# Depthwise convolution on TensorE with 64 channels doubled in time: four tiles there, three on VectorE

## The chip, the cores and the metric

The kernel runs on one core of one Trainium2 chip. The metric is device time in microseconds (us) of one launch, the median of several runs. Durations inside the kernel come from one profiled execution, whose own time stands beside the median below.

## The reference

Two layers run over 256 latent tokens of width 1024 (batch 1), with 256 context tokens that share the weights. Each layer is a gated feed-forward block, a mixer, and a second feed-forward block; after each of them comes a residual and a LayerNorm. The mixer of layer 0 is attention with pooling; that of layer 1 is the convolution module, and only there does the change lie:

```python
a, g = jnp.split(h @ w_c1 + b_c1, 2, axis=-1)
z = a * jax.nn.sigmoid(g)
z = lax.conv_general_dilated(z, w_dw[:, None, :], window_strides=(1,), padding=[(15, 15)], ..., feature_group_count=1024) + b_dw
z = jax.nn.silu(layer_norm(z, ln_g, ln_b))
return z @ w_c2 + b_c2
```

The middle step is a depthwise convolution: 31 taps over time, each of the 1024 channels by itself, in float32.

## The kernel before

**Weights.** Every large weight is loaded as float32 in pieces of 1 MB (`raw`, three buffers) by DMAs that SyncE issues, and split into a high part on ScalarE (`wh`, line 133) and a low part on VectorE, or for some pieces on GpSimd (`wl`, line 134). Each product is three matmuls on TensorE (lines 196 to 198). A `raw` buffer is loaded again when both parts of its old content have been made.

**Convolution stage (from line 864).** The 1024 channels are eight tiles `j` of 128 channels; channels lie on partitions, the 256 tokens along a row. The first product and `glu` (line 884) fill `zp[:, j, :]`, which has 15 zeros on both sides. Then the tiles part ways:

- `DVE_CONV`, tiles 0, 2, 3, 4: VectorE adds up 31 scaled, shifted copies in PSUM (`dve_tap`, lines 904 and 907).
- `POOL_CONV`, tile 1: ScalarE makes 31 scaled copies (`product`, lines 917 and 921, in buffers `pd`), GpSimd adds them (`add_up`, line 925).
- `PE_CONV`, tiles 5, 6, 7: for each tap ScalarE makes a diagonal matrix `dg` (line 986), and TensorE multiplies it with the shifted row of 256 tokens and adds up in the PSUM tile `pc` (line 987). ScalarE copies `pc` to `cv` with the bias (line 990).

`back(j)` (line 929) transposes a finished tile so that tokens lie on partitions (`cvt`, one PSUM tile for each 128 tokens and each half of the channels, line 935), and VectorE takes statistics of it (`ln_part`, line 299). `BACK` says behind which tap matmul the transposes of which tiles are queued; `back_after(last, 7)` is the last. Then come the mean and variance (line 1001), the inverse root on GpSimd (line 1003), the scaling to `yn` (line 1011), transposes back (line 1018), SiLU into `cv` (line 1020), the split into `XH`, `XL`, and the second product. Three rows `bcr` (bias b_c2), `lnr[0]`, `lnr[1]` are loaded at the start of the stage; lines 994 to 996 scale `bcr` and add it to `lnr[1]`, and lines 1006 and 1007 apply them to the residual `h`.

**Order of the work.** The framework writes out the order of each engine's instructions, and of SyncE's DMAs, ahead of time: of the instructions whose inputs and buffers are ready in its own model of the time, the one that stands first in the program comes first. So an instruction can overtake one that stands ahead of it in the program. On the chip each queue then goes strictly in that order: a waiting instruction holds all behind it. `tc.issue_after(x)` puts instructions behind `x` on the same engine. PSUM tiles are tracked by bank: a write into one part of a tile waits for reads of another part that stand ahead in the program.

Of the kernel before, what the change touches and what calls it, by code (L numbers as in the profile page):

```python
# [9 lines left out]
F32 = mybir.dt.float32  # L10
F32R = mybir.dt.float32r
AF = mybir.ActivationFunctionType
# [4 lines left out]
P = 128  # L17
D = 1024
KT = D // P
SEQ = 256  # L20
# [6 lines left out]
TAPS = 31  # L27
HALO = TAPS // 2
# [3 lines left out]
NSPARE = 4  # L32
HP = 700

DVE_CONV = (0, 2, 3, 4)
POOL_CONV = 1
PE_CONV = (5, 6, 7)
PLO = range(9, 24)

BACK = {(5, 30): (0,), (6, 30): (1, 2, 5), (7, 20): (3, 6), (7, 30): (4,)}  # L40


CO = {}
_n = 0
for _name, _w in (("c", 8), ("cc", 8), ("lng", 48), ("lnb", 48), ("cvg", 8), ("cvb", 8), ("bc1", 16), ("bdw", 8),
                  ("psc", 4), ("sub", 1), ("bad", 9 * 8 * DEPTH)):
    CO[_name] = _n
    _n += _w
# [4 lines left out]
def body(ctx: ExitStack, tc: tile.TileContext, out, a):  # L53
    nc = tc.nc
    act, dve, pool, pe = nc.scalar, nc.vector, nc.gpsimd, nc.tensor
# [12 lines left out]
    def mmt(name):  # L68
        return mmp.tile([P, 512], F32, tag="mm", name=name)

    def trt(name):
        return trp.tile([P, 512], F32, tag="tr", name=name)
# [4 lines left out]
    ident = const.tile([P, P], F32, name="ident")  # L77
# [5 lines left out]
    def col(name, i=0, n=1):  # L83
        return cols[:, CO[name] + i: CO[name] + i + n]
# [13 lines left out]
    taken = [0]  # L98
# [23 lines left out]
    def spare(pool, q0, n, tag, **kw):  # L122
        for q in range(q0, q0 + n):
            alt[q] = lambda name: pool.tile([P, 1024], F32R, tag=tag or name[:2] + "x", name=name, **kw)
# [12 lines left out]
    def wnext(ahead=AHEAD):  # L137
        q = taken[0]
        taken[0] += 1
        pump_load(qmap[q][0] + 3)  # L140
        with behind_x():
            pump_split(q + ahead)
        return ready[q]
# [152 lines left out]
    def ln_part(key, i, n, src):  # L296
        if key not in bst:
            bst[key] = tp.tile([P, n, 6], F32, tag="bst", name=f"bst{key}")
        dve.bn_stats(bst[key][:, i, :], src)
# [177 lines left out]
    with ExitStack() as st0:  # L477
# [29 lines left out]
        for ch in range(2):  # L507
            cs = slice(ch * 4, ch * 4 + 4)
            for v in range(2):
# [3 lines left out]
                for q in range(4):  # L513
                    aw = sp.tile([P, 1024], F32, tag="aw", name=f"aw{v}{ch}{q}", bufs=8)
                    nc.sync.dma_start(aw, a["wst"][v, ch, q // 2, :, (q % 2) * 1024:(q % 2 + 1) * 1024])
                    for kk in range(2):
                        k = q * 2 + kk
                        src = aw[:, kk * 512:(kk + 1) * 512]
# [17 lines left out]
                tr = trt(f"sttr{v}{ch}")  # L536
# [55 lines left out]
    with ExitStack() as st2:  # L592
# [44 lines left out]
        for g, win in enumerate(WINS):  # L637
            src = (SA, SB)[g % 2]
            o = 8 - win // 2
# [224 lines left out]
    with ExitStack() as st3:  # L864
        cp = st3.enter_context(tc.tile_pool(name="cp", bufs=1))
        c2 = st3.enter_context(tc.tile_pool(name="c2", bufs=2))
        xmp[:] = c2, 2
        bcr = cp.tile([P, D], F32, name="bcr")
        nc.sync.dma_start(bcr, a["b_c2"][0].partition_broadcast(P))
        lnr = [cp.tile([P, D], F32, name=f"clnr{j}") for j in range(2)]  # L870
        for j, key in enumerate(("ln_g", "ln_b")):
            nc.sync.dma_start(lnr[j], a[key][1, 0].partition_broadcast(P))
        G = mrow[1, 5, 0]
        wd = cp.tile([P, 8 * TAPS], F32, name="wd")
        nc.sync.dma_start(wd, a["wdw"])
        warm = cp.tile([P, 1], F32, name="warm")
        zp = cp.tile([P, KT, SEQ + 2 * HALO], F32, name="zp")
        for o in (0, HALO + SEQ):
            pool.memset(zp[:, :, o:o + HALO], 0.0)
        cv = cp.tile([P, KT, SEQ], F32, name="cv")  # L880
        taps = []
# [9 lines left out]
        pds = []  # L891
        last_add = [None]

        def dve_tap(j, tap):
            w = wd[:, j * TAPS + tap:j * TAPS + tap + 1]
            if tap == 0:
                i = DVE_CONV.index(j)
                if i % 2 == 0:
                    accs[j] = adp.tile([P, 512], F32, tag="ad", name="acc01") if i == 0 else mmt(f"acc{j}")
                else:  # L900
                    accs[j] = accs[DVE_CONV[i - 1]][:, SEQ:]
            acc = accs[j][:, 0:SEQ]
            if tap == 0:
                dve.tensor_scalar(acc, zp[:, j, 0:SEQ], w, col("bdw", j), ALU.mult, ALU.add)
            else:
                dst = cv[:, j, :] if tap == TAPS - 1 else acc
                dve.scalar_tensor_tensor(dst, zp[:, j, tap:tap + SEQ], w, acc, ALU.mult, ALU.add)

        def tapstep(n):
            for _ in range(min(n, len(taps))):  # L910
                dve_tap(*taps.pop(0))


        def product(j, tap):
            w = wd[:, j * TAPS + tap:j * TAPS + tap + 1]
            if tap == 0:
                act.activation(cv[:, j, :], zp[:, j, 0:SEQ], AF.Identity, bias=col("bdw", j), scale=w)
                return
            if tap % 4 == 1:
                pds.append(c2.tile([P, 4, SEQ], F32, tag=("whx", "wlx")[len(pds) % 2], name=f"pd{j}{tap}", bufs=4))  # L920
            act.activation(pds[-1][:, (tap - 1) % 4, :], zp[:, j, tap:tap + SEQ], AF.Copy, scale=w)

        def add_up(j):
# [3 lines left out]
        cvt = {}  # L927

        def back(j):

            half = j // 4
            for t in range(2):
                if (t, half) not in cvt:
                    cvt[t, half] = mmt(f"cvt{t}{half}")
                pe.transpose(cvt[t, half][:, (j % 4) * P:(j % 4 + 1) * P], cv[:, j, t * P:(t + 1) * P], ident)
                if j == 3:
                    ln_part(f"c{t}", 0, 5, cvt[t, 0])
                elif j > 3:
                    ln_part(f"c{t}", j - 3, 5, cvt[t, 1][:, (j % 4) * P:(j % 4 + 1) * P])
# [4 lines left out]
        for t in range(2):  # L944
# [5 lines left out]
            tr = trt(f"cltr{t}")  # L950
# [6 lines left out]
        for j in range(2, 8):  # L957
            ps = mmt(f"c1{j}")
            for u in range(2):
                wh, wl = wnext(min(5, q0 + 16 - taken[0]))  # L960
                for k in range(KT):
                    mm3(ps[:, u * SEQ:(u + 1) * SEQ], wh[:, k * P:(k + 1) * P], wl[:, k * P:(k + 1) * P],
                        XH[:, k, 0:SEQ], XL[:, k, 0:SEQ], k == 0, k == KT - 1)
                tapstep(4)
                for _ in range(3):
                    if prods:
                        product(*prods.pop(0))
            glu(j, ps[:, 0:SEQ], ps[:, SEQ:])
            if j in DVE_CONV:
                taps += [(j, tap) for tap in range(TAPS)]  # L970
        with tc.issue_after(sgi[0].ins):
            warm_ins = act.activation(warm, mhalf[:, 0:1], AF.Silu)
        with tc.issue_after(lo_ins[q0 + 15].ins):
# [2 lines left out]
        def back_after(ins, *js):  # L976
            with tc.issue_after(ins.ins):
                for j in js:
                    back(j)

        for j in PE_CONV:
            pc = trt(f"pc{j}")[:, 0:SEQ]
            for tap in range(TAPS):
                dg = c2.tile([P, P], F32, tag="dg", name=f"dg{j}{tap}", bufs=8)
                o = j * TAPS + tap
                act.activation(dg, ident, AF.Copy, scale=wd[:, o:o + 1])
                last = pe.matmul(pc, dg, zp[:, j, tap:tap + SEQ], start=tap == 0, stop=tap == TAPS - 1)
                if (j, tap) in BACK:
                    back_after(last, *BACK[j, tap])
            act.activation(cv[:, j, :], pc, AF.Identity, bias=col("bdw", j))  # L990
        back_after(last, 7)

        with tc.issue_after(warm_ins.ins), tc.issue_after(last_add[0].ins):
            act.mul(bcr, bcr, 1.0 / ALPHA)
# [18 lines left out]
        for j0 in range(0, 8, 2):  # L1013
            tr = trt(f"ytr{j0}")
            for j in (j0, j0 + 1):
                for t in range(2):
                    o = (j - j0) * SEQ + t * P
                    pe.transpose(tr[:, o:o + P], yn[t][:, j * P:(j + 1) * P], ident)
            for j in (j0, j0 + 1):
                act.activation(cv[:, j, :], tr[:, (j - j0) * SEQ:(j - j0 + 1) * SEQ], AF.Silu, bias=col("cvb", j), scale=col("cvg", j))  # L1020
            sl = slice(j0, j0 + 2)
            split(XH[:, sl, SEQ:2 * SEQ], XL[:, sl, SEQ:2 * SEQ], cv[:, sl, :])
        spare(c2, taken[0] + 4, 4, None, bufs=4)
        for n in range(2):
            pss = [mmt(f"c2{n}{t}") for t in range(2)]
            with tc.issue_after(warm_ins.ins):
# [19 lines left out]
def _layout(i):  # L1046
    import numpy as np
    f = lambda v: np.asarray(v)
    ar = np.ascontiguousarray
    L = DEPTH  # L1050
    o = {}

    def vec(v):
        return f(v).reshape(-1, P).T
# [3 lines left out]
    GATES = (2, 5, 8)  # L1058
    by = lambda b, v: b.reshape(P, 8).T if v in GATES else b.reshape(8, P)
    bad = np.concatenate([by(b_ada[l, v], v).T for l in range(L) for v in range(9)], axis=1)  # L1060
    o["cols"] = ar(np.concatenate([
        vec(i["c"]), vec(i["c_ctx"]), vec(i["ln_g"]), vec(i["ln_b"]), vec(i["conv_ln_g"]), vec(i["conv_ln_b"]),
        vec(i["b_c1"]), vec(i["b_dw"]), vec(i["pool_scale"]), vec(i["subln_g"]), bad], axis=1))
    o["wdw"] = ar(f(i["w_dw"])[0].reshape(TAPS, 8, P).transpose(2, 1, 0).reshape(P, 8 * TAPS))
    x, ctx = f(i["x"])[0], f(i["ctx"])[0]
    o["x"], o["ctx"] = ar(x), ar(ctx)
    o["xT"] = ar(np.stack([v.reshape(SEQ, KT, P).transpose(2, 1, 0).reshape(P, KT * SEQ) for v in (x, ctx)]))
# [2 lines left out]
    wt = wa.transpose(0, 2, 3, 1)  # L1070
# [55 lines left out]
```

## Time and profile before

| | us |
|---|---|
| runs: median (lowest to highest of 3) | 1250.89 (1249.99 to 1252.77) |
| profiled execution, its time | 1249.67 |
| profiled execution, span from first to last instruction | 1247.9 |
| tap matmuls on TensorE, first start to last start | 970.6 to 1013.0 |
| first mean and variance (line 1001) | 1015.68 |

The span leaves out what lies ahead of the first and behind the last instruction (1249.67 - 1247.9 = 1.8 us). The profile names TensorE's matmuls PE, its weight loads PEld, VectorE DVE, ScalarE ACT, GpSimd POOL and SyncE SP; a name that ends in q is that engine's queue. A float32 matmul shows as two matmuls and two weight loads, so that the 3 x 31 = 93 tap matmuls are 186 rows of each kind; they are called passes here. Matmuls overlap one another: their pace is the distance from start to start, not the length of one.

### The profile page before, as it was taken

What the parts mean: (1) busy time and instruction counts of PE and PEld (TensorE: products, weight loads), DVE (VectorE), ACT (ScalarE), POOL (GpSimd) and SP (SyncE); (2) the same over time, 40 slices, a digit from 0 to 9 for tenths busy, and PEclk for the clock granted to TensorE, in tenths of its full rate; (3) what the DMA queues carried; (4) which work ended last, traced back from release to release, by engine and by line L of the source; (5) the groups of instructions that cost most, each with busy time, mean ns of one, the idle gap of its engine ahead of it and who ended that gap; (6) DMA issues with size and microseconds to landing.
All of it is one profiled execution on the core that took longest, in us unless ns stands there. A gap on an engine that the chain in (4) does not pass through costs nothing.

```text
span 1247.9 us, 17504 instructions
## 1 busy us (share of the span) xinstructions
PE 1201.0 (96%) x6886; PEld 1031.9 (83%) x6886; DVE 889.1 (71%) x1278; ACT 520.8 (42%) x790; POOL 257.6 (21%) x231
## 2 busy tenths in 40 slices
PE   7999999999999899999999999999999989999997
PEld 1688888888887777779998879999879867999985
DVE  6889986833337966778776678878659876875554
ACT  2532222322223535654444444434448863544431
POOL 0010201121004741024001014201017961320000
PEclk9999999999999999999999999999999989999999
DMA  9798788732232441349986649998735141985550
GB/s 364 280 373 259 268 287 297 253 103 99 85 118 78 132 169 68 135 147 369 328 289 234 227 160 339 337 324 291 269 134 203 34 135 41 364 293 183 182 186 35
DMA packets 63748, 264.32 MB, mean 212 GB/s; under 512 B 5937, under 2 KB 6705, under 8 KB 56241
## 3 DMA queue, kind: packets, MB, share of 16 engines
q1 hardware_dynamic: 60128, 251.11, 57.2%
q0 software_dynamic: 3536, 12.09, 2.9%
q8 instruction: 54, 0.88, 0.3%
q14 instruction: 30, 0.24, 0.1%
HBM read 262.10 MB, written 1.08 MB: 211 GB/s over the span
## 4 chain that ended last, share of the span: by engine, by line
PE 80%; DVE 9%; ACT 4%; POOL 2%; issue 2%; DMA 2%; SPq 0%; DVEq 0%; POOLq 0%; ACTq 0%
PE uf L196 8%; PE uf L198 8%; PE uf L197 8%; PE gf L197 8%; PE gf L198 8%; PE gf L196 8%; PE of L196 7%; PE of L198 7%; PE of L197 7%; PE c L196 1%; DVE wl L134 1%; PE c L197 1%; PE c L198 1%; PE st L520 1%; POOL XL L203 1%
## 5 line engine op out<-in xcount | busy, mean ns | idle before, releaser
L134 DVE TENSOR_TENSOR wl<-raw,wh 128x1024 fp32r<-128x1024 f32 x298 | 377.7, 1283 | 163.5 <-ACT wh L133 162.9
L133 ACT CAST wh<-raw 128x1024 fp32r<-128x1024 f32 x313 | 321.6, 1046 | 392.4 <-PE of L198 128.0
L196 PE MATMUL gf<-XH,wh 128*128 128x256 f32 (+1 forms) x656 | 204.6, 312 | 0.3 <-ACT XH L203 0.3
L198 PE MATMUL gf<-XH,wl 128*128 128x256 f32 (+1 forms) x656 | 204.7, 312 | 0.0
L197 PE MATMUL gf<-XL,wh 128*128 128x256 f32 (+1 forms) x656 | 204.6, 312 | 0.0
L196 PE MATMUL uf<-XH,wh 128*128 128x256 f32 (+1 forms) x656 | 204.4, 312 | 0.0
L197 PE MATMUL uf<-XL,wh 128*128 128x256 f32 (+1 forms) x656 | 204.4, 312 | 0.0
L198 PE MATMUL uf<-XH,wl 128*128 128x256 f32 (+1 forms) x656 | 204.4, 312 | 0.0
L238 DVE SCALAR_TENSOR_TENSOR ada<-ada,crow0ada 128x1024 f32<-128x1024 f32 x104 | 128.6, 1250 | 67.0 <-DMA ada<-in_wada 66.8
L197 PE MATMUL of<-wl,GHf 128*128 128x512 f32 x344 | 134.0, 389 | 0.0
L198 PE MATMUL of<-wh,GLf 128*128 128x512 f32 x344 | 133.9, 389 | 0.0
L196 PE MATMUL of<-wh,GHf 128*128 128x512 f32 x344 | 133.9, 389 | 0.0
L196 PEld LDWEIGHTS gf<-XH,wh 128*128 128x128 f32 x656 | 124.1, 189 | 8.4 <-issue 0.9
L197 PEld LDWEIGHTS gf<-XL,wh 128*128 128x128 f32 x656 | 124.1, 189 | 7.4 <-DVE XL L203 0.4
L198 PEld LDWEIGHTS gf<-XH,wl 128*128 128x128 f32 x656 | 124.2, 189 | 6.9
L196 PEld LDWEIGHTS uf<-XH,wh 128*128 128x128 f32 x656 | 124.2, 189 | 6.8
L198 PEld LDWEIGHTS uf<-XH,wl 128*128 128x128 f32 x656 | 124.0, 189 | 6.9
L197 PEld LDWEIGHTS uf<-XL,wh 128*128 128x128 f32 x656 | 124.1, 189 | 6.8
L246 POOL TENSOR_TENSOR m<-m,cols 128x8 f32<-128x8 f32 x19 | 19.1, 1006 | 336.6 <-DVE ada L238 214.2
L198 PEld LDWEIGHTS of<-wh,GLf 128*128 128x128 f32 x344 | 64.6, 188 | 13.5
L197 PEld LDWEIGHTS of<-wl,GHf 128*128 128x128 f32 x344 | 64.6, 188 | 13.3
L196 PEld LDWEIGHTS of<-wh,GHf 128*128 128x128 f32 x344 | 64.6, 188 | 13.2
(293 smaller groups left out, 1858.7 us busy)
## 6 DMA issues: line engine op xcount, KB each, us to landing
raw<-in_wfi SPq DMA_DIRECT2D x82, 1024.0 KB, 6.9
ada<-in_wada SPq DMA_DIRECT2D x128, 512.0 KB, 5.6
raw<-in_wfo SPq DMA_DIRECT2D x40, 1024.0 KB, 4.9
raw<-in_wc SPq DMA_DIRECT2D x10, 1024.0 KB, 5.1
aw<-in_wst SPq DMA_DIRECT2D x16, 512.0 KB, 8.2
raw<-in_wfl SPq DMA_DIRECT2D x6, 1024.0 KB, 5.3
raw<-in_wfo SPq DMA_DIRECT2D x8, 512.0 KB, 3.6
raw<-in_wqk SPq DMA_DIRECT2D x4, 1024.0 KB, 5.4
```

The lines of the kernel that those rows point to most:

```text
L133: act.copy(wh[:, :w], r[:, off:off + w])
L134: lo_ins[q] = (pool if q in pool_lo else dve).tensor_tensor(wl[:, :w], r[:, off:off + w], wh[:, :w].bitcast(F32), ALU.subtract)
L196: pe.matmul(ps, lh, rh, start=first, stop=False)
L197: pe.matmul(ps, lh, rl, start=False, stop=False)
L198: last_mm[0] = pe.matmul(ps, ll, rh, start=False, stop=last)
L203: return act.copy(dh, src), eng.tensor_tensor(dl, src, dh.bitcast(F32), ALU.subtract)
L238: dve.scalar_tensor_tensor(st["raw"] if s == streams[-1] else crow["junk"], st["raw"], 1.0, crow[s], ALU.mult, ALU.mult, accum_out=mcol[l, ...
L246: pool.tensor_tensor(m, m, col("bad", (l * 9 + v) * 8, 8), ALU.add)
L520: started = pe.matmul(ps[0:2, :], scv[:, :, k], src, start=started is None, stop=not dq and k == KT - 1)
```

## The change

Tile 4 moves from VectorE to TensorE, so that TensorE has tiles 4 to 7 and VectorE 0, 2 and 3. On TensorE a tile is treated in two groups `g` of 64 channels. `double(j)` copies the 64 rows twice into `zd`: to partitions 0 to 63 as they are, and to partitions 64 to 127 shifted by one token (four DMAs a tile, from SBUF to SBUF, on SyncE's queue; three `zd` buffers). A matrix of 128 x 128 then takes two taps of 64 channels and makes two outputs of each channel, the even token on columns 0 to 63 and the odd one on 64 to 127. A group needs 16 matmuls, each over 128 columns (every second token: a step of two floats), where 31 matmuls over 256 columns were needed for a tile. The matrices `wcv` are laid out by the host and loaded in 16 pieces of 512 KB, eight matrices each, through five buffers; a piece's load is issued when its buffer's old piece has been used. The `dg` matrices are gone.

After that, TensorE's tiles stand in `cv` with even tokens on partitions 0 to 63 and odd ones on 64 to 127, and are transposed in 64-row blocks (four transposes a tile instead of two); other tiles are read with a step of two, so that `cvt[0]` has even and `cvt[1]` odd tokens; line 1020's successor puts them in order again. `bcr` and the two `lnr` rows are loaded through the `wcv` buffers, behind the last pieces. `pd` has three buffers of each kind instead of four, and three weight parts instead of four go into them later (`spare`). `BACK` is new.

```diff
-DVE_CONV = (0, 2, 3, 4)
+DVE_CONV = (0, 2, 3)
 POOL_CONV = 1
-PE_CONV = (5, 6, 7)
+PE_CONV = (4, 5, 6, 7)
...
-BACK = {(5, 30): (0,), (6, 30): (1, 2, 5), (7, 20): (3, 6), (7, 30): (4,)}
+BACK = {5: (0,), 6: (2, 1, 4), 7: (3, 5, 6)}
...
-        bcr = cp.tile([P, D], F32, name="bcr")
-        nc.sync.dma_start(bcr, a["b_c2"][0].partition_broadcast(P))
-        lnr = [cp.tile([P, D], F32, name=f"clnr{j}") for j in range(2)]
-        for j, key in enumerate(("ln_g", "ln_b")):
-            nc.sync.dma_start(lnr[j], a[key][1, 0].partition_broadcast(P))
...
+        zd, wcv, wcvs = {}, [], [(n, g) for n in range(len(PE_CONV)) for g in range(4)]
+
+        def double(j):
+            zd[j] = c2.tile([P, 2, SEQ + 2 * HALO], F32, tag="zd", bufs=3, name=f"zd{j}")
+            for g in range(2):
+                for u in range(2):
+                    w = SEQ + 2 * HALO - u
+                    nc.sync.dma_start(zd[j][u * 64:(u + 1) * 64, g, 0:w], zp[g * 64:(g + 1) * 64, j, u:u + w])
+
+        def wcv_load():
+            if wcvs:
+                n, g = wcvs.pop(0)
+                wcv.append(c2.tile([P, D], F32, tag="wcv", bufs=5, name=f"wcv{n}{g}"))
+                nc.sync.dma_start(wcv[-1], a["wcv"][n, g])
...
+                o = (j % 4) * P
+                if j in PE_CONV:
+                    ts = slice(t * 64, (t + 1) * 64)
+                    for g in range(2):
+                        pe.transpose(cvt[t, half][:, o + g * 64:o + (g + 1) * 64], cvp[j][ts, g, :], ident[ts, ts])
+                else:
+                    pe.transpose(cvt[t, half][:, o:o + P], cv[:, j, :].rearrange("p (i b) -> p b i", b=2)[:, t, :], ident)
...
             if j in DVE_CONV:
                 taps += [(j, tap) for tap in range(TAPS)]
+            else:
+                double(j)
+                wcv_load()
+                if j == PE_CONV[0]:
+                    wcv_load()
...
-        for j in PE_CONV:
+
+        cvp = {}
+        for n, j in enumerate(PE_CONV):
             pc = trt(f"pc{j}")[:, 0:SEQ]
-            for tap in range(TAPS):
-                dg = c2.tile([P, P], F32, tag="dg", name=f"dg{j}{tap}", bufs=8)
-                o = j * TAPS + tap
-                act.activation(dg, ident, AF.Copy, scale=wd[:, o:o + 1])
-                last = pe.matmul(pc, dg, zp[:, j, tap:tap + SEQ], start=tap == 0, stop=tap == TAPS - 1)
-                if (j, tap) in BACK:
-                    back_after(last, *BACK[j, tap])
-            act.activation(cv[:, j, :], pc, AF.Identity, bias=col("bdw", j))
+            cvp[j] = cv[:, j, :].rearrange("p (g i) -> p g i", g=2)
+            for g in range(2):
+                for tap in range(16):
+                    if tap % 8 == 0:
+                        wt = wcv.pop(0)
+                        wcv_load()
+                    z2 = zd[j][:, g, 2 * tap:2 * tap + SEQ].rearrange("p (i b) -> p b i", b=2)[:, 0, :]
+                    last = pe.matmul(pc[:, g * P:(g + 1) * P], wt[:, tap % 8 * P:(tap % 8 + 1) * P], z2, start=tap == 0, stop=tap == 15)
+                act.activation(cvp[j][:, g, :], pc[:, g * P:(g + 1) * P], AF.Identity, bias=col("bd2", 2 * j + g))
+            if j in BACK:
+                back_after(last, *BACK[j])
         back_after(last, 7)
+        bcr, *lnr = [c2.tile([P, D], F32, tag="wcv", bufs=5, name=n) for n in ("bcr", "clnr0", "clnr1")]
+        for row, src in ((lnr[0], a["ln_g"][1, 0]), (bcr, a["b_c2"][0]), (lnr[1], a["ln_b"][1, 0])):
+            nc.sync.dma_start(row, src.partition_broadcast(P))
```

## Rows read from the trace of the kernel before

**Rows 1.** Profile page, each engine's busy time, share of the span, instructions.

```profile
PE 1201.0 (96%) x6886; PEld 1031.9 (83%) x6886; DVE 889.1 (71%) x1278; ACT 520.8 (42%) x790; POOL 257.6 (21%) x231
```

**Rows 2.** Stretches: busy us of PE, PEld, DVE, ACT, POOL; PEclk, DMA share, GB/s.

```profile
936.00:971.00 35.00, 35.00 (x293) 34.97 (x292) 31.84 (x66) 26.10 (x57) 27.75 (x22) 1.00 0.53 181
971.00:1013.00 42.00, 41.77 (x197) 35.44 (x196) 35.99 (x74) 37.85 (x101) 34.39 (x26) 1.00 0.34 109
```

**Rows 3.** PE in order of time: start, length, line, shape, count.

```profile
970.36 0.28 PE L197 MATMUL c<-XL,wh 128*128 128x256 f32 x1
970.48 0.28 PE L198 MATMUL c<-XH,wl 128*128 128x256 f32 x1
970.61 13.55 PE L987 MATMUL pc<-zp,dg 128*128 128x256 f32 x62
...
997.60 0.82 PE L935 MATMUL cvt<-ident,cv 128*128 128x128 f32 x6
...
1008.88 4.49 PE L987 MATMUL pc<-zp,dg 128*128 128x256 f32 x20
1014.12 0.53 PE L935 MATMUL cvt<-ident,cv 128*128 128x128 f32 x2 [0.76 <-DVE bstc L299]
1014.93 0.43 PE L935 MATMUL cvt<-ident,cv 128*128 128x128 f32 x2 [0.29 <-DVE bstc L299]
```

**Rows 4.** DVE in order of time, 987 to 1016 us.

```profile
987.27 0.48 DVE L907 SCALAR_TENSOR_TENSOR cv<-zp,wd,acc 128x256 f32<-128x256 f32 x1
...
1012.80 0.46 DVE L907 SCALAR_TENSOR_TENSOR cv<-zp,wd,acc 128x256 f32<-128x256 f32 x1
1013.18 1.08 DVE L299 BATCH_NORM_STATS2 bstc<-cvt 128x6 f32<-128x512 f32 x3
1014.49 0.50 DVE L299 BATCH_NORM_STATS2 bstc<-cvt 128x6 f32<-128x128 f32 x2 [0.22 <-PE cvt L935]
...
1015.68 0.42 DVE L1001 BATCH_NORM_AGGREGATE cmv<-bstc 128x2 f32<-128x30 f32 x2
```

**Rows 5.** Line 987, tap matmuls and their weight loads: min/median/max ns.

```profile
L987 PEld LDWEIGHTS pc<-zp,dg x186: 186/189/192, 970.5 to 1012.8; 128*128 128x128 f32 x186
L987 PE MATMUL pc<-zp,dg x186: 377/378/483, 970.6 to 1013.0; 128*128 128x256 f32 x186
```

**Rows 6.** Groups by line and form, 936 to 1016 us.

```profile
L986 ACT ACTIVATE dg<-ident,wd 128x128 f32<-128x128 f32 x93 | 28.8, 390 | 0.0
L196 PEld LDWEIGHTS c<-XH,wh 128*128 128x128 f32 x95 | 18.2, 192 | 0.0
L886 ACT ACTIVATE csg<-cltr,cols 128x128 f32<-128x128 f32 x2 | 0.7, 360 | 0.0
```

**Rows 7.** POOL in order of time, 958 to 1017 us.

```profile
958.95 24.29 POOL L925 TENSOR_TENSOR cv<-cv,pd 128x256 f32<-128x256 f32 x30
983.20 2.36 POOL L995 TENSOR_TENSOR bcr<-bcr,grow 128x1024 f32<-128x1024 f32 x1
...
987.95 18.70 POOL L134 TENSOR_TENSOR wl<-raw,wh 128x1024 fp32r<-128x1024 f32 x8
1016.39 0.71 POOL L1003 TENSOR_TENSOR crs<-crs,mhalf 128x2 f32<-128x2 f32 x1 [9.74 <-DVE crs L1002]
```

**Rows 8.** DMA issues: count, KB each, median us to landing.

```profile
ada<-in_wada SPq DMA_DIRECT2D x128, 512.0 KB, 5.6
...
bcr<-in_b_c SPq DMA_DIRECT2D x1, 512.0 KB, 3.5
...
clnr<-in_ln_b SPq DMA_DIRECT2D x1, 512.0 KB, 6.4
```

**Rows 9.** Busy time by stretch again, DMA share and GB/s last.

```profile
940.00:945.00 5.00, 5.00 (x44) 5.00 (x43) 4.75 (x11) 5.00 (x13) 1.93 (x2) 1.00 0.89 314
...
985.00:990.00 5.00, 5.00 (x25) 4.38 (x24) 4.65 (x11) 5.00 (x15) 4.92 (x3) 1.00 0.00 2
```

**Rows 10.** SyncE's queue, 895 to 1060 us: its waits, longest in total first.

```profile
SPq L112 <- POOL wl L134: 64.6, 8, 33.3
```

More of the change, by code (lines that the diff above doesn't have):

```diff
@@ L33 @@
 HP = 700
-DVE_CONV = (0, 2, 3, 4)
+DVE_CONV = (0, 2, 3)
 POOL_CONV = 1
-PE_CONV = (5, 6, 7)
+PE_CONV = (4, 5, 6, 7)
 PLO = range(9, 24)
-BACK = {(5, 30): (0,), (6, 30): (1, 2, 5), (7, 20): (3, 6), (7, 30): (4,)}
+BACK = {5: (0,), 6: (2, 1, 4), 7: (3, 5, 6)}
 CO = {}
 _n = 0
-for _name, _w in (("c", 8), ("cc", 8), ("lng", 48), ("lnb", 48), ("cvg", 8), ("cvb", 8), ("bc1", 16), ("bdw", 8),
+for _name, _w in (("c", 8), ("cc", 8), ("lng", 48), ("lnb", 48), ("cvg", 8), ("cvb", 8), ("bc1", 16), ("bdw", 8), ("bd2", 16),
                   ("psc", 4), ("sub", 1), ("bad", 9 * 8 * DEPTH)):
@@ L919, in product @@
             if tap % 4 == 1:
-                pds.append(c2.tile([P, 4, SEQ], F32, tag=("whx", "wlx")[len(pds) % 2], name=f"pd{j}{tap}", bufs=4))
+                pds.append(c2.tile([P, 4, SEQ], F32, tag=("whx", "wlx")[len(pds) % 2], name=f"pd{j}{tap}", bufs=3))
             act.activation(pds[-1][:, (tap - 1) % 4, :], zp[:, j, tap:tap + SEQ], AF.Copy, scale=w)
@@ L934, in back @@
                     cvt[t, half] = mmt(f"cvt{t}{half}")
-                pe.transpose(cvt[t, half][:, (j % 4) * P:(j % 4 + 1) * P], cv[:, j, t * P:(t + 1) * P], ident)
+                o = (j % 4) * P
[5 more added lines that the diff above has]
+                    pe.transpose(cvt[t, half][:, o:o + P], cv[:, j, :].rearrange("p (i b) -> p b i", b=2)[:, t, :], ident)
                 if j == 3:
@@ L1019, in body @@
             for j in (j0, j0 + 1):
-                act.activation(cv[:, j, :], tr[:, (j - j0) * SEQ:(j - j0 + 1) * SEQ], AF.Silu, bias=col("cvb", j), scale=col("cvg", j))
+                act.activation(cv[:, j, :].rearrange("p (i b) -> p b i", b=2),
+                               tr[:, (j - j0) * SEQ:(j - j0 + 1) * SEQ].rearrange("p (b i) -> p b i", b=2),
+                               AF.Silu, bias=col("cvb", j), scale=col("cvg", j))
             sl = slice(j0, j0 + 2)
             split(XH[:, sl, SEQ:2 * SEQ], XL[:, sl, SEQ:2 * SEQ], cv[:, sl, :])
-        spare(c2, taken[0] + 4, 4, None, bufs=4)
+        spare(c2, taken[0] + 4, 3, None, bufs=3)
         for n in range(2):
@@ L1060, in _layout @@
     bad = np.concatenate([by(b_ada[l, v], v).T for l in range(L) for v in range(9)], axis=1)
+    bd2 = np.tile(f(i["b_dw"]).reshape(8, 2, 1, 64), (1, 1, 2, 1)).reshape(16, P).T
     o["cols"] = ar(np.concatenate([
         vec(i["c"]), vec(i["c_ctx"]), vec(i["ln_g"]), vec(i["ln_b"]), vec(i["conv_ln_g"]), vec(i["conv_ln_b"]),
-        vec(i["b_c1"]), vec(i["b_dw"]), vec(i["pool_scale"]), vec(i["subln_g"]), bad], axis=1))
+        vec(i["b_c1"]), vec(i["b_dw"]), bd2, vec(i["pool_scale"]), vec(i["subln_g"]), bad], axis=1))
     o["wdw"] = ar(f(i["w_dw"])[0].reshape(TAPS, 8, P).transpose(2, 1, 0).reshape(P, 8 * TAPS))
+    taps = np.zeros((D, TAPS + 2), np.float32)
+    taps[:, 1:-1] = f(i["w_dw"])[0].T
+    wcv = np.zeros((len(PE_CONV), 2, 2, 64, 16, 2, 64), np.float32)
+    ch = np.arange(64)
+    for n, j in enumerate(PE_CONV):
+        for g in range(2):
+            for u in range(2):
+                for v in range(2):
+                    c0 = j * P + g * 64
+                    wcv[n, g, u, ch, :, v, ch] = taps[c0:c0 + 64, 1 + u - v:1 + u - v + 31:2]
+    o["wcv"] = ar(wcv.reshape(len(PE_CONV), 2, P, 2, D).transpose(0, 1, 3, 2, 4).reshape(len(PE_CONV), 4, P, D))
     x, ctx = f(i["x"])[0], f(i["ctx"])[0]
```

## The prediction

> **What bounds the kernel now.** I read the page first: TensorE is busy 96% of the span [rows 1], so a stage is shortened only where TensorE waits or does work that can go. The change lies in one stage, so I read the stretches next. In 936 to 971 us (first product of the convolution stage) TensorE is busy all the time; in 971 to 1013 us too, but there VectorE (36 of 42 us), ScalarE (38) and GpSimd (34) are nearly full as well [rows 2]. To see which ends last I read each engine in order of time. TensorE goes from the first product straight into the tap matmuls at 970.61 and ends the last at 1008.88 + 4.49 = 1013.37 [rows 3]. VectorE ends its last tap, of tile 4, at 1012.80 + 0.46 = 1013.26 [rows 4]: a tie. The tail behind both, two more tiles transposed and measured in turn, brings the first mean and variance at 1015.68 [rows 4], 45.1 us after 970.61. What comes later (inverse root, scaling, second product, last feed-forward block) hangs on that moment, so I take a gain there as a gain of the whole.
>
> **Tap matmuls.** Before, 62 passes of a tile take 13.55 us, the last of them 0.378 [rows 3, 5]: (13.55 - 0.38)/61 = 0.216 us from start to start. 186 x 0.216 = 40.2 us; 12 transposes among them (three groups, of which the middle one stands in the rows) at (0.82 - 0.27)/5 = 0.11 [rows 3] are 1.3; the other 1.3 of 42.8 is switching, a short wait for `dg` and the end of the last pass.
> After, 4 tiles x 2 groups x 16 matmuls x 2 passes = 256 passes over 128 columns. No row shows that form. Below, its nearest row is the transpose, also float32 with 128 columns: 0.11, that is 28.2 us. The nearest row with the same kind of weight load is a pass of the first product, 0.12 from start to start [rows 3]: its load of 128 x 128 is listed with 192 ns [rows 6], that of a tap pass with 189 [rows 5]. Half of 0.216 is 0.108 of streaming, so I expect the load to be about as long as the streaming, as in that row, and take 0.12: 256 x 0.12 = 30.7 us. Above lie 0.189, if the listed load were the pace (48.4 us), and 0.216, if a step of two floats in the moving operand cost as much as reading all 256 columns (55.3 us). 0.216 is also what a pass would take if load and streaming followed each other, 0.108 each. Both come back as rivals; loads listed with 192 ns at a pace of 120 speak against the first and against loads that follow, no row against the dear step.
> The Trainium skill (TensorE: Matmul & The Clock Gate, Part 3, The mechanism) says that a weight load overlaps matmuls in flight only where the row group differs. Our loads fill all rows, so by that rule load and streaming would follow each other; with its 107 ns for 128 columns (LDWEIGHTS) a pass would be some 0.21 us, an estimate from the page, and the taps 55 us. The trace disagrees for the first product: same rows, pace 0.12.
> The Trainium skill (SBUF — State Buffer, Door 1, on 16-byte lines) says that steps up to four float32 are free as long as two accesses hit a line; by it our step of two costs nothing. No run here shows it.
>
> **Between and around them.** Transposes queued among the passes: two behind tile 5, eight behind tile 6, 10 x 0.11 = 1.1 us. Switching as before, 1.0. New is a turn inside each tile: both groups lie in one bank of `pc`, and the second group's first write waits until ScalarE has read the first. That such waits exist shows in the two transposes that wait for VectorE's statistics of other columns of the same tile [rows 3]. Price: the end of the last pass about 0.15, the copy 0.36 [rows 6], two handovers 0.1: 0.6 us, up to 1.6 where a cast stands ahead on ScalarE. The planned order can fill the turn with the next tile's first passes, except in tile 7: between 0.6 and 2.4 us in all, I take 1.2. Sum: 30.7 + 1.1 + 1.0 + 1.2 = 34.0, so the last pass ends near 1004.6 instead of 1013.4.
>
> **Tail.** Before: 2.3 us from the last pass to the mean. Now tiles 3, 5, 6 and 7 stand behind the last pass. A tile that shares its bank with the one before takes a round of 0.8 us (transposes at 1014.12 and 1014.93 [rows 3], statistics at 1014.49 and 1015.27 [rows 4]). First transposes 0.35, tile 3's two wide statistics 1.2 (three statistics, one wide, take 1.08 [rows 4]), tile 5 0.5, tiles 6 and 7 0.8 each, 0.2 handover: 3.9. Mean at 1008.5, 7.2 us earlier.
>
> **What is removed at no gain.** 93 `dg` activations, 28.8 us of ScalarE [rows 6], and VectorE's tile 4 from 987.8 to 1013.3 [rows 4]. They lie beside TensorE's taps. But both had to go: with tile 4 still on VectorE the stage would stay at 1013. VectorE's third tile is done at 987.75 [rows 4], GpSimd's tile at 983.24 [rows 7]: covered by 17 us and more. Next late would be GpSimd.
>
> **Loads.** 16 pieces of 512 KB and 16 small copies join SyncE's queue. The first five pieces need no old piece gone and can land during the first product. Then the load of piece n+5 goes out when piece n is used, and has four pieces of 16 x 0.12 = 1.92 us, 7.7 us, to land; 512 KB take a median 5.6 (3.5 for `bcr`) [rows 8]. Need: 0.524 MB per 1.92 us = 273 GB/s, beside a stretch in which DMA stood still (2 GB/s in 985 to 990) and under the 314 GB/s of 940 to 945 [rows 9]. Cost nothing, with 2.1 us to spare; every us later than that stalls TensorE one for one. The copies into `zd` are four short issues a tile; tile 7's waits for tile 4's buffer, 64 x 0.12 = 7.7 us into the taps, and is needed two tiles, 15 us, after that: nothing.
>
> **GpSimd.** `bcr` and the two rows now land late: the last one's buffer is free two pieces before the end (about 1000.7), its load takes 3.5 to 6.4 [rows 8], so line 996 ends near 1009; the inverse root, ready at 1009.1, may wait. Between 0 and 2.4 us (one such step [rows 7]), I take 0.5. In exchange the eight low parts can start 4.7 us earlier, at 983.2 [rows 7]. `pd` with three buffers: ScalarE's last products wait for GpSimd's first additions, from 959 on [rows 7], in a stretch in which ScalarE is busy 26 of 35 us [rows 2]; nothing. One weight part of the next block loses its early buffer and is split during the second product instead: nothing, or one subtract (2.34) if it lands in the tail.
>
> **Sum.** 7.2 - 0.5 = 6.7 us. The profiled execution took 1249.67, so 1243.0; the median of the runs lies 1.2 above it, so I say 1244.
>
> **Rivals.**
> - *SyncE's order (the other side).* One queue holds casts' loads and pieces. The last `w_c2` load waited 33.3 us for GpSimd [rows 10]; after the change GpSimd frees its buffer near 983.2 + 2 x 2.34 = 988 [rows 7]. If the order written ahead puts it in front of pieces that TensorE needs from 980 on, all behind it wait. An issue that is late by more than 2.1 us costs the rest; from 2.1 + 6.7 = 8.8 us on the kernel is slower. Worst, from piece 5 on: it lands at 988 + 5.6 = 993.6 and is needed at 970.6 + 5 x 1.92 = 980.2; 13.4 lost, 6.7 slower, 1258. For it: one queue, and such a wait is there already. Against: the order is made by readiness, and a buffer's release on a busy GpSimd comes late in any model. A few us late: gain 2 to 5, about 1247.5.
> - *GpSimd's order.* If the `bcr` steps stay ahead of the eight low parts (as at 983.20 and 987.95 [rows 7]) the parts start near 1008 and the inverse root may stand behind k of them at 2.34 us each: from k = 3 the gain is gone, k = 8 gives 1262. For it: that order stands in the trace. Against: it came about with `bcr` loaded long before; with a late load the low parts are ready first.
> - *A pass costs more than 0.12,* by a load that is not hidden or by the step. From 0.146 us (6.7/256 more) the gain is gone; 0.189 gives 17.7 - 6.7 = 11 us slower, 1262; 0.216 gives 1269.
> - *It moves nothing,* since the splits for the second product end the stage near the old time: 1250. For it: GpSimd makes low parts until 1006.65 before [rows 7], as late as the new last pass. Against: it starts them 4.7 us earlier now, and needs none of them for the mean.
>
> **Chances.** Forecast (1239 to 1246.5) 0.62; SyncE 0.18 (half of it still faster, 0.06 slower); GpSimd 0.08 (half slower, half same); dearer pass 0.07, slower; nothing moves 0.05. A measurement tells 0.2% (2.5 us) from no change. Faster 0.71, same 0.12, slower 0.17. Range: at the low end 0.11 a pass, no turns, the old tail, no wait on GpSimd: 2.5 + 0.6 + 1.6 + 0.5 = 5 lower, 1239. The high end takes in late pieces and small misorders, 1251; the dear pass stays outside.
>
> **What the next profile would show.** Right: 256 passes from about 970.6 at 0.12, the first mean near 1008.5, no waits of TensorE's loads for `wcv`. Wrong: a pace near 0.19 or 0.216; gaps of TensorE ended by a DMA of `wcv` with a long wait of SyncE ahead of them; the inverse root waiting behind low parts; turns of over a microsecond in each tile. A mean that comes 7 us earlier with an unchanged total would say that what follows does not hang on it.

## The result, and the profile after

The changed kernel took 1263.45 us (median of 6 runs, 1259.07 to 1265.23) against 1251.83 (median of 6, 1249.99 to 1255.49): a ratio of 1.0083, interval 1.006 to 1.0106. It is slower; I had said 1244, and given "slower" 17 in 100. The profiled execution took 1259.07 us, 9.4 more than the profiled one of before. It was the fastest of the six; what made the others up to 6.2 us longer shows in no profile.

TensorE in order of time shows where they went (start, length, line, shape, count, and in brackets the idle time before and what ended it):

```profile
971.79 11.32 PE L1013 MATMUL pc<-zd,wcv 128*128 128x128 f32 x96
996.27 5.27 PE L1013 MATMUL pc<-zd,wcv 128*128 128x128 f32 x32 [13.16 <-ACT cv L1014]
...
1001.61 3.84 PE L1013 MATMUL pc<-zd,wcv 128*128 128x128 f32 x32
1005.90 3.95 PE L1013 MATMUL pc<-zd,wcv 128*128 128x128 f32 x32 [0.46 <-ACT cv L1014]
...
1014.93 3.95 PE L1013 MATMUL pc<-zd,wcv 128*128 128x128 f32 x32 [0.46 <-ACT cv L1014]
```

96 passes run at the pace of the forecast, (11.32 - 0.28)/95 = 0.116 us. Then TensorE stands 13.16 us, and what ends the stand is a copy of ScalarE, the one that reads tile 5's first group out of the bank into which the second group is to be written. After it the pace is there again, but for the first 32 passes. The last pass ends at 1018.88; forecast 1004.6.

Why was that copy late? ScalarE in order of time:

```profile
980.16 0.37 ACT L1014 ACTIVATE cv<-pc,cols 128x128 f32<-128x128 f32 x1 [0.25 <-PE pc L1013]
994.90 1.05 ACT L133 CAST wh<-raw 128x1024 fp32r<-128x1024 f32 x1 [14.38 <-DMA raw<-in_wc]
995.85 0.36 ACT L1014 ACTIVATE cv<-pc,cols 128x128 f32<-128x128 f32 x1
```

A 0.36 us copy stands behind a cast, and the cast waits 14.38 us for a weight load. The load is in SyncE's queue:

```profile
973.82 2.17 SPq L921 DMA_DIRECT2D wcv<-in_wcv  x2
988.91 0.33 SPq L112 DMA_DIRECT2D raw<-in_wc  x1
989.34 2.38 SPq L915 DMA_DIRECT2D zd<-zp  x4
991.77 16.60 SPq L921 DMA_DIRECT2D wcv<-in_wcv  x9
```

It goes out at 988.91, ahead of tile 7's copies and of pieces 7 to 15. The chain that ended last tells what it waited for:

```profile
984.23 4.66 POOL wl L134 x2
988.89 0.02 issue
988.91 5.92 DMA raw<-in_wc
...
994.90 1.05 ACT wh L133
995.95 0.28 ACT cv L1014
996.22 0.04 issue
996.27 0.79 PE pc L1013 x2
```

So the chain is: GpSimd adds up its tile until 984.23, makes two low parts (4.66), which frees the load's buffer at 988.89; the load takes 5.92; then cast, copy, passes. SyncE had waited 12.8 us at that load (its waits, answering to [rows 10]):

```profile
SPq L112 <- POOL wl L134: 25.5, 5, 12.8
```

The stretches that answer to [rows 2] show the empty time (columns as there):

```profile
936.00:971.00 35.00, 35.00 (x291) 34.85 (x290) 28.50 (x57) 24.96 (x49) 26.68 (x21) 1.00 0.73 258
971.00:1013.00 42.00, 28.39 (x231) 27.73 (x231) 20.94 (x52) 11.60 (x17) 30.59 (x25) 0.84 0.58 184
```

Every engine has slack in 971 to 1013, and TensorE is busy 28.39 of 42 us where it was busy 41.77. VectorE in order of time gives the end of the stage:

```profile
1022.25 1.23 DVE L134 TENSOR_TENSOR wl<-raw,wh 128x1024 fp32r<-128x1024 f32 x1 [1.54 <-ACT wh L133]
...
1024.67 0.42 DVE L1030 BATCH_NORM_AGGREGATE cmv<-bstc 128x2 f32<-128x30 f32 x2
```

The first mean comes at 1024.67, 9.0 us after the 1015.68 of before [rows 4]: nearly the whole loss of 9.4. A second planned order costs time in the first of these lines: VectorE waits for the cast of a load of the next block with the last statistics queued behind it, so the tail from the last pass to the mean is 5.8 us. It is 5.7 and 6.0 us in experiments 5 and 7, which keep that order, and 3.2 in experiments 1 and 6, which do not.

### The profile page after: what moved, and what is told of

Its sections match the earlier page's. It is cut to its first block, busy times and chain, and to the rows that moved or that the text cites. A ratio compares the mean times of both kernels' runs of the same rounds, so it can differ in the third digit from the quotient of the medians.

```text
span 1257.3 us, 17600 instructions
## 1 busy us (share of the span) xinstructions
PE 1194.1 (95%) x6964; PEld 1030.4 (82%) x6964; DVE 876.3 (70%) x1247; ACT 496.7 (40%) x702; POOL 255.7 (20%) x231
## 4 chain that ended last, share of the span: by engine, by line
PE 82%; DVE 8%; ACT 3%; POOL 2%; DMA 2%; issue 2%; SPq 0%; DVEq 0%; POOLq 0%; ACTq 0%
PE uf L198 8%; PE uf L197 8%; PE uf L196 8%; PE gf L197 8%; PE gf L198 8%; PE gf L196 8%; PE of L198 7%; PE of L196 7%; PE of L197 7%; PE c L198 1%; PE c L197 1%; PE c L196 1%; PE pc L1013 1%; PE st L520 1%; DVE wl L134 1%
## 5 line engine op out<-in xcount | busy, mean ns | idle before, releaser
L238 DVE SCALAR_TENSOR_TENSOR ada<-ada,crow0ada 128x1024 f32<-128x1024 f32 x104 | 131.3, 1272 | 62.3 <-DMA ada<-in_wada 62.0
```

Of the source, the lines that this page charges most:

```text
L238: dve.scalar_tensor_tensor(st["raw"] if s == streams[-1] else crow["junk"], st["raw"], 1.0, crow[s], ALU.mult, ALU.mult, accum_out=mcol[l, ...
```

## The experiments

**The theory.** The order written ahead put the last `w_c2` load in front of nine pieces on SyncE, and its cast in front of the copy on ScalarE, though its buffer comes free only at 988.9 on a busy GpSimd. The terms for passes, turns and tail were right. **Rivals.** Only one of the two queues made the loss; the copies on ScalarE are too dear in themselves; the second half of the loss lies in something that the matrices' traffic slows. Where an edit moved more in an engine's planned order than it was meant to, it is said. Edits are shown in short: bookkeeping is left out, and a comment names the place.

**1. The load held back.** The last `w_c2` load and the loads after it go out behind the last piece on SyncE. Its cast then moves behind the copies too, and on VectorE the subtract of the next block moves from in front of the last statistics to behind the scaling.

```
 def wcv_load():
-    nc.sync.dma_start(wcv[-1], a["wcv"][n, g])
+    raw_hold[0] = nc.sync.dma_start(wcv[-1], a["wcv"][n, g])
...
 # in pump_load, for the last w_c2 load and all loads after it
+with tc.issue_after(raw_hold[0].ins):
     nc.sync.dma_start(dst, src)
```

> The change, with one edge more: the load of the last w_c2 piece (and the weight loads after it) is put behind the last load of tap matrices in SyncE's order. Theory A (in the order written ahead this load stands in front of matrices that TensorE needs, and its cast in front of a copy that TensorE needs, while its buffer waits for GpSimd): the gap of 13.2 us inside the taps goes, the last pass ends near 1006 instead of 1019, the first mean comes near 1011, and the time is some 13 us below that of the change, 1246 beside 1251 for the kernel before. Theory B (loads of 512 KB for 1.9 us of work can't be kept up with): TensorE still waits between the pieces, total 1255 or more. Theory C (what follows the stage doesn't hang on it): last pass earlier, total as the change.

Measured: 1247.63 us (median of 7), ratio 0.9968, interval 0.9955 to 0.998. The stand is gone; TensorE of this kernel in order of time:

```profile
971.87 11.32 PE L1017 MATMUL pc<-zd,wcv 128*128 128x128 f32 x96
983.64 3.95 PE L1017 MATMUL pc<-zd,wcv 128*128 128x128 f32 x32 [0.46 <-ACT cv L1018]
...
1000.99 3.95 PE L1017 MATMUL pc<-zd,wcv 128*128 128x128 f32 x32 [0.46 <-ACT cv L1018]
```

The last pass ends at 1004.94 and the first mean comes at 1008.14; the forecast had 1004.6 and 1008.5. A copy that comes on time costs a turn of 0.46 us, so the copies are not too dear in themselves; and with the same matrices loaded beside them the passes keep their pace. Yet the total fell by only 3.9 us, not 6.7. GpSimd and VectorE show the rest, still in this kernel:

```profile
1003.92 4.70 POOL L138 TENSOR_TENSOR wl<-raw,wh 128x1024 fp32r<-128x1024 f32 x2 [5.44 <-ACT wh L137]
1008.58 2.35 POOL L1029 TENSOR_TENSOR bcr<-bcr,grow 128x1024 f32<-128x1024 f32 x1
1011.01 2.34 POOL L1030 TENSOR_TENSOR clnr<-clnr,bcr 128x1024 f32<-128x1024 f32 x1
1013.30 0.71 POOL L1037 TENSOR_TENSOR crs<-crs,mhalf 128x2 f32<-128x2 f32 x1
```

```profile
1008.14 0.43 DVE L1035 BATCH_NORM_AGGREGATE cmv<-bstc 128x2 f32<-128x30 f32 x2
...
1014.04 2.97 DVE L1045 TENSOR_SCALAR yn<-cvt,cmv,crs 128x512 f32<-128x512 f32 x4 [3.09 <-POOL crs L1037]
```

The inverse root (the 128x2 step) stands behind two late low parts and two steps on rows. It ends 1013.30 + 0.71 - 1008.14 = 5.9 us after the start of the mean, where before it ended 1016.39 + 0.71 - 1015.68 = 1.4 after [rows 4, 7]: 4.5 us lost in that place. An inverse root behind low parts is what the prediction's second rival feared, though with the row steps in front of the parts and not behind them.

**2. The copies on VectorE.** The eight copies out of `pc` move from ScalarE to VectorE.

```
-act.activation(cvp[j][:, g, :], pc[:, g * P:(g + 1) * P], AF.Identity, bias=col("bd2", 2 * j + g))
+dve.tensor_scalar(cvp[j][:, g, :], pc[:, g * P:(g + 1) * P], col("bd2", 2 * j + g), None, ALU.add)
```

> The change, with the copies of the tap sums out of PSUM on VectorE instead of ScalarE; SyncE's order is as in the change. This takes away ScalarE's part alone. Theory A: the tap matrices of piece 7 are still loaded only behind the late weight load, near 992, so TensorE goes on near 996.5 as before; time within 3 us of the change (1256 to 1263). Rival A1 (only ScalarE's queue holds TensorE): the gap of 13.2 us goes, about 1246.

Measured: 1266.19 us, ratio 1.0114 (1.0092 to 1.0135). It does not isolate anything: the planned order changed with it, on SyncE too. TensorE stands 6.35 us for a copy that is queued behind VectorE's own taps, and 7.11 us for one that is queued behind a subtract that waits 10.85 us for ScalarE. What it shows is only that another engine's queue can hold the copies in the same way.

**3. A cast forced ahead of the copy, with the load held.** The copy of tile 5's first group is kept behind the cast, in the kernel of experiment 1; for that, the casts stand earlier in the program.

```
+if (n, g) == (1, 0):
+    spare(c2, q0 + 20, 3, None, bufs=3)
+    pump_split(q0 + 23)
+with tc.issue_after(hi_ins[q0 + 22].ins):   # only for (n, g) == (1, 0)
     act.activation(cvp[j][:, g, :], pc[:, g * P:(g + 1) * P], ...)
```

> SyncE's part alone is taken away: the late weight load stands behind the eleventh load of tap matrices, but the copy of tile 5's first group on ScalarE is put behind the cast of that weight load. Theory A (each of the two waits is enough by itself): TensorE can only fill in tile 6's first group (32 passes, 3.8 us) and then stands until the copy near 996; a gap of 8 to 10 us, total 1253 to 1258. Rival A2 (only SyncE's order holds TensorE): no gap, about 1246.

Measured: 1265.51 us, ratio 1.011 (1.0078 to 1.0141). Inconclusive: the earlier place also put casts ahead of tile 7's sigmoid, which came 9.83 us late to VectorE. Experiments 5 and 6 ask the same question without that.

**4. Own PSUM tiles, earlier transposes.** Experiment 1, and each group gets a PSUM tile of its own; the transposes of tiles 3 and 5 are queued behind tile 6's passes and not behind tile 7's.

```
-BACK = {5: (0,), 6: (2, 1, 4), 7: (3, 5, 6)}
+BACK = {5: (0,), 6: (2, 1, 3, 4, 5), 7: (6,)}
...
+pc = trt(f"pc{j}{g}")[:, 0:P]
```

> As e1, and each group of 64 channels has a PSUM tile of its own (no wait for ScalarE between the groups of a tile), and the transposes of tiles 3 and 5 stand behind tile 6 instead of 7. Theory A with the tail as the forecast priced it: the waits of 0.46 us before second groups go (1 us in all) and the tail from last pass to first mean falls by 1.5 us or so; total 2 to 3 us below e1, about 1243. If the tail is set by GpSimd and the late rows, total as e1.

Measured: 1246.31 us, ratio 0.9963 (0.9946 to 0.9979). The turns are gone (128 passes in one row of 14.86 us) and the mean comes at 1005.16, 3.0 us before that of experiment 1, but the total is the same within what can be told. VectorE waits 5.39 us for the inverse root, which stands behind the same four steps:

```profile
1012.16 2.97 DVE L1045 TENSOR_SCALAR yn<-cvt,cmv,crs 128x512 f32<-128x512 f32 x4 [5.39 <-POOL crs L1037]
```

**5. SyncE's order alone.** The changed kernel with only the two casts of the last load moved behind tile 5's copies. On SyncE, TensorE, VectorE and GpSimd every instruction stands where it stood.

```
 # in pump_split, for the two casts of the last w_c2 load
+with tc.issue_after(copy_of_tile5_group1.ins):
     act.copy(wh[:, :w], r[:, off:off + w])
```

> The changed kernel with SyncE's order as it is (the last load of w_c2 ahead of tile 7's copies and of matrix pieces 7 to 15), and only ScalarE's order mended: the two casts of that load stand behind both copies of tile 5. The theory (each of the two queues by itself is enough): TensorE gets on by the 16 passes of piece 6, to about 985.5, and then stands until piece 7 lands, issued at about 991.8 and there 4 to 5 us later, so until about 996.5; it has 16 passes (2 us) fewer to do then than the changed kernel, so 1255 to 1262 us, and the first passes' wait ended by a DMA of a piece, not by ScalarE. The rival (ScalarE's order alone made the loss): no stand of more than 1 us, 1246 to 1249 us.

Measured: 1260.8 us, ratio 1.009 (1.0063 to 1.0116). TensorE in order of time:

```profile
982.70 2.11 PE L1017 MATMUL pc<-zd,wcv 128*128 128x128 f32 x16 [0.46 <-ACT cv L1018]
996.32 3.78 PE L1017 MATMUL pc<-zd,wcv 128*128 128x128 f32 x16 [11.51 <-DMA wcv<-in_wcv]
```

The copy is on time (0.46), 16 passes run, and then TensorE stands 11.51 us for piece 7, which waits on SyncE behind the load. The moment at which it goes on, 996.3, is that of the changed kernel.

**6. ScalarE's order alone.** On SyncE the last load stands behind tile 7's copies and pieces 7 to 10, and the next block's loads behind all pieces; on ScalarE its cast stays ahead of the copy. The passes go tile by tile here, and the cast and subtract of the next block move ahead of the last statistics and no longer stand between them.

```
+if (n, g) == (2, 2):
+    raw_hold[0] = ins        # piece 10; the last w_c2 load goes behind it
...
+tc.add_manual_dep(copy_of_tile5_group0, cast.ins.name, order only)
```

> The reverse: on SyncE all copies of tile 7 and pieces 7 to 11 go out ahead of the last load of w_c2, and the loads of the next stage behind all pieces, but on ScalarE the cast of that load is held ahead of the copy of tile 5's first group, as in the changed kernel; the passes go tile by tile. The theory (each queue by itself is enough): the load still starts only when GpSimd has freed its buffer at about 988.9, lands some 6 us later, and the copy follows its cast at about 995.9, so TensorE stands 13 us as in the changed kernel: 1256 to 1264 us. The rival (the pieces' lateness behind the load made the loss, the cast only shared it): under 1250 us.

Measured: 1258.76 us, ratio 1.0063 (1.0043 to 1.0082). ScalarE, then TensorE:

```profile
993.56 1.05 ACT L138 CAST wh<-raw 128x1024 fp32r<-128x1024 f32 x1 [13.51 <-DMA raw<-in_wc]
994.51 0.36 ACT L1029 ACTIVATE cv<-pc,cols 128x128 f32<-128x128 f32 x1
```

```profile
994.92 6.33 PE L1028 MATMUL pc<-zd,wcv 128*128 128x128 f32 x32 [11.61 <-ACT cv L1029]
```

Pieces were there; the copy was not. From the start of the first pass to the end of the last it is 47.1 us in the changed kernel, 47.1 in experiment 5, 47.3 here and 33.1 in experiment 1. So each queue alone is enough for nearly the whole stand, and to mend only one of them gains next to nothing. The rivals that name a single queue are out.

**7. The buffer free earlier.** The changed kernel with both queues as they are (the load's two casts swap places on ScalarE); on GpSimd the two low parts that free the load's buffer go ahead of the last nine additions. The other low parts moved too, in between the additions.

```
 # in add_up: addition 21 and those after it go behind the second low part
+tc.add_manual_dep(addition_21, lo_ins[q0 + 17].ins.name, order only)
```

> The changed kernel with the orders of SyncE, TensorE, VectorE as they are and the cast of the last w_c2 load still ahead of the copy of tile 5's first group on ScalarE (the load's two casts swap places); only GpSimd is changed: the two low parts that free the load's buffer stand ahead of its last nine additions of tile 3 and not behind them. The theory: the buffer is free at about 981 in place of 988.9, the load starts and lands as much earlier (about 987), the copy ends near 988.4, so TensorE stands about 5.5 us in place of 13.2 and the time falls by 7 to 8, to 1252 to 1256 us. The rival (the stand comes from the order of the queues however early the buffer is free, for instance since DMA is slower with all pieces under way): a stand of more than 10 us and over 1257 us. Under 1249 would say that the load is not on the path at all.

Measured: 1253.37 us (median of 10), ratio 1.0012 (1.0 to 1.0024). GpSimd, SyncE and TensorE, one line each:

```profile
977.51 4.74 POOL L135 TENSOR_TENSOR wl<-raw,wh 128x1024 fp32r<-128x1024 f32 x2
```

```profile
982.28 0.33 SPq L112 DMA_DIRECT2D raw<-in_wc  x1
```

```profile
989.86 6.54 PE L1019 MATMUL pc<-zd,wcv 128*128 128x128 f32 x32 [5.39 <-ACT cv L1020]
```

The stand falls from 13.16 to 5.39 us, 7.8 less. The buffer is free 6.6 us earlier (982.25 against 988.89) and the passes begin 1.4 us later (973.15 against 971.79): 8.0 together. So with the orders of SyncE and TensorE untouched, the stand follows the moment at which GpSimd frees the buffer. That is where the chain begins.

The totals come out less neatly. In the profiled executions the way from the first pass to the mean is 6.3 us shorter (1019.76 - 973.15 = 46.6 against 52.9), since the passes after the stand are slower by 1.3 (6.54 against 5.27); less the later start that is 4.9, and the time is 3.3 less (1255.76). The medians differ by 10.1, but the profiled execution was the fastest of the changed kernel's six and the slowest of this one's ten. What part of either difference is the stand's stays open.

**8 and 9. The inverse root first.** Experiments 1 and 4 again, with the two steps on rows behind the inverse root on GpSimd. In experiment 8 no other engine's order changes; in 9 one cast and its subtract also move, behind the scaling.

```
-with tc.issue_after(warm_ins.ins), tc.issue_after(last_add[0].ins):
+with tc.issue_after(warm_ins.ins):
     act.mul(bcr, bcr, 1.0 / ALPHA)
-    pool.tensor_tensor(bcr, bcr, G, ALU.mult)
-    pool.tensor_tensor(lnr[1], lnr[1], bcr, ALU.add)
...
 with tc.issue_after(last_pow[0].ins):
+    pool.tensor_tensor(bcr, bcr, G, ALU.mult)
+    pool.tensor_tensor(lnr[1], lnr[1], bcr, ALU.add)
```

> The kernel in which the last loads are held behind the pieces, with one change on GpSimd alone: the two steps on b_c2 and on the shift row (2.35 us each) stand behind the inverse root of the norm and not ahead of it. If GpSimd's order took what the forecast's sum missed there, the normalised tiles start about 0.5 us after the mean and its bias step, near 1009.9 in place of 1014.0, so 3 to 4 us less than the kernel without this change: about 1244, the forecast's own figure. If something else (the second product's matrices, the residual rows h, which now come 4.7 us later) was as late, nothing is gained: 1247 to 1248.

> The same GpSimd step on the kernel that also has a PSUM tile for each group and most of the turns ahead of the last passes. There the inverse root waited 5.4 us behind low parts and rows. If GpSimd's order is what holds it, the normalised tiles start near 1007 in place of 1012.2 and the time is 1246.3 less 5, about 1241; if the last low parts of w_c2 (ready near 1006.7) or h are as late, 1244 to 1246.

Measured, on top of experiment 1: 1245.17 us, ratio 0.9949 (0.9933 to 0.9965). On top of experiment 4: 1241.17 us, ratio 0.9926 (0.9906 to 0.9946), the fastest of all kernels here. In the first of the two, GpSimd and then VectorE:

```profile
1002.91 4.70 POOL L138 TENSOR_TENSOR wl<-raw,wh 128x1024 fp32r<-128x1024 f32 x2 [5.34 <-ACT wh L137]
1008.00 0.71 POOL L1035 TENSOR_TENSOR crs<-crs,mhalf 128x2 f32<-128x2 f32 x1 [0.38 <-DVE crs L1034]
```

```profile
1007.29 0.42 DVE L1033 BATCH_NORM_AGGREGATE cmv<-bstc 128x2 f32<-128x30 f32 x2
...
1008.74 2.97 DVE L1045 TENSOR_SCALAR yn<-cvt,cmv,crs 128x512 f32<-128x512 f32 x4 [0.82 <-POOL crs L1035]
```

From the mean's start to the root's end it is 1.4 us again, as before. The scaling begins 5.3 us earlier than in experiment 1 and the span is 4.0 shorter (1241.8 against 1245.8); the medians differ by 2.5. On top of experiment 4 it is 4.9 in the spans (1240.0 against 1244.9) and 5.1 in the medians. That experiment 4 had gained nothing over experiment 1 was GpSimd's order: with it mended the same step is worth 4.0 us (1245.17 against 1241.17).

## Why the prediction was wrong

**The failed step** is the sentence "Cost nothing, with 2.1 us to spare" under loads, together with the price of a turn, "up to 1.6 where a cast stands ahead on ScalarE". The first took each piece's load to go out as soon as its own buffer is free, with nothing held in front of it; the second took a cast ahead of a copy to cost its own length. Measured, piece 7 went out at 991.77 behind a load that SyncE held for 12.8 us, the cast ahead of the copy waited 14.38, and TensorE stood 13.16. A load in front of the pieces costs as long as its buffer is not free, and a cast in front of a copy as long as its load has not landed.

The prediction had SyncE's half of this as a rival, at 0.18 (0.06 for slower): a buffer free near 988 (988.9 measured), 13.4 us lost (13.16), 6.7 slower. That 13.4 comes so near is in part luck. It was the worst case, from piece 5 on, held on SyncE alone; in fact pieces 5 and 6 went out in time at 973.82, the stand began behind pass 96, and what ended it was a copy on ScalarE, which the rival left out. The kernel was 10.4 us slower by the ratio and 9.4 between the profiled executions, not 6.7. What I held against it, "the order is made by readiness, and a buffer's release on a busy GpSimd comes late in any model", was an argument with no row behind it, while the row for it, 33.3 us of SyncE waiting at such a load [rows 10], was on the page. Before, that wait cost nothing, as TensorE needed nothing behind it. And the cast on ScalarE makes the same stand by itself (experiment 6), so two of the planned orders had to be right, not one.

**The account.** From the first pass to the mean the changed kernel takes 1024.67 - 971.79 = 52.9 us, experiment 1 takes 36.3, before 45.1. The 16.6 between the first two are 12.7 of stand (13.16 less a turn of 0.46), 1.3 for the 32 slow passes after it (5.27 against 3.95) and 2.6 of tail (5.8 against 3.2, the subtract in front of the statistics): 16.6. Against before it is 7.8 longer and starts 1.2 later, which makes the 9.0.

**The pass, 0.12.** Right: 0.116, 29.7 us for 256. The rival of a dearer pass is out. The form's row, its weight loads and its passes (min, median, max in ns):

```profile
L1013 PEld LDWEIGHTS pc<-zd,wcv x256: 186/188/333, 971.7 to 1018.5; 128*128 128x128 f32 x128
L1013 PE MATMUL pc<-zd,wcv x256: 273/276/581, 971.8 to 1018.6; 128*128 128x128 f32 x128
```

Loads listed with 188 ns over all rows keep a pace of 116, so load and streaming overlap. How far can be estimated from two rows: 256 columns take 0.216 and 128 take 0.116, so 128 columns more cost 0.100, and 0.016 us of a pass is left for all that is not streaming. The Trainium skill (TensorE: Matmul & The Clock Gate, Part 3, The mechanism) allows the overlap, in its list, only where the row group differs, and in the paragraph above also for a load into the background weight buffer; the trace disagrees with the list taken alone. A step of two floats costs nothing that shows, where reading all 256 columns would have shown as 0.216. Here the Trainium skill (SBUF — State Buffer, Door 1, on 16-byte lines) and the trace agree.

**Turns, 1.2.** Right: three of 0.46 in experiment 1, 1.4 us. **Tail, 3.9.** 3.2 in experiment 1. **Mean at 1008.5.** 1008.14 there. **The mean carries the total.** Right in size: 9.0 later gave 9.4 more in the changed kernel. In the other direction only once the root followed the mean: in experiment 8 the mean is 8.4 us earlier than before and the profiled time 6.1 shorter (1249.67 less 1243.59). Behind the scaling the second product takes 28.4 us there from its first pass to its last, and 25.8 before.

**GpSimd, 0.5.** Wrong for the forecast's own course. In the changed kernel the root ends 1.8 us after the mean's start, so 0.4 lost; but there the mean is late. With the stand gone it was 4.5 lost, above my bound of 2.4, since two low parts and both steps on rows stood ahead; part of that is my hold, which made the low parts late. With the order mended (experiment 8) the gain is 6.4 us by the ratio (1251.3 x 0.0051) against the forecast sum of 6.7. That they agree is in part luck: the mean came 8.4 us earlier and not 7.2, and in the profiled executions 2.3 of it were lost behind the mean where 0.5 was forecast.

**Bandwidth of the pieces.** Right: 512 KB land in a median 4.9 us (page of the changed kernel, against 5.6 assumed), and in experiment 1 no pass waits for a piece. Only the moment of issue was wrong.

```profile
wcv<-in_wcv SPq DMA_DIRECT2D x16, 512.0 KB, 4.9
```

**What stays open.** In each of the profiles with the change the passes begin 0.3 to 3.1 us later than the 970.61 of before. The first product's stretch moves 258 GB/s where it moved 181 [rows 2]; that the pieces' traffic is the cause was not tried.

## What to carry to other kernels

An instruction put ahead of others in an in-order queue is priced by the moment at which it can start, not by its length: for each queue that the change adds work to, list what stands in front and when the slowest engine frees its buffer. Where each of two queues holds the same work, as here, mending one gains next to nothing, and each must be looked at before a term is set to nothing. A gain at one engine (here the earlier mean) is only a gain once the next step's queue has been followed to the operation that takes it up.

## What the runs showed of the hardware

The clock that TensorE is granted falls when it stands, and the work behind a stand pays for it. In the changed kernel these are the stand and the passes after it (columns as in [rows 2]):

```profile
983.00:996.00 13.00, 0.11 (x1) 0.00 (x0) 8.45 (x19) 1.10 (x2) 12.92 (x8) 0.60 0.45 139
996.30:1001.50 5.20, 5.20 (x34) 5.20 (x35) 0.00 (x0) 0.85 (x1) 5.20 (x3) 0.72 0.91 321
1001.60:1005.40 3.80, 3.80 (x34) 3.64 (x32) 0.00 (x0) 0.34 (x1) 1.24 (x1) 1.00 0.77 252
```

The granted clock is a mean of 0.60 in the stand and 0.72 in the first 32 passes, between the two levels (0.5 and 1, 1.2 and 2.4 GHz), and 1.00 after them. 32 passes took 5.27 us here, 6.33 after a stand of 11.61 (experiment 6, clock 0.59) and 6.54 after one of 5.39 (experiment 7, clock 0.56), where 3.8 to 3.95 is usual: of these three, the shortest stand was paid for most. The same thing took part of the gain in experiment 8. The second product starts 5.3 us earlier than in experiment 1, but its first passes, in 1013 to 1020, run at 0.50:

```profile
1013.30:1020.30 7.00, 5.57 (x15) 4.18 (x15) 7.00 (x4) 3.46 (x7) 7.00 (x4) 0.50 0.02 7
1020.40:1024.00 3.60, 3.60 (x17) 2.97 (x16) 3.60 (x2) 1.68 (x3) 3.60 (x2) 0.99 0.00 0
```

From the first pass that reads `XL`, the low part of the split input, seven passes take 3.15 us there (1017.25 to 1020.40) and 1.71 in experiment 1 (1022.54 to 1024.25), so that of the 5.3 us 4.0 are left at the last pass (1041.7 against 1045.7).
